# The spatial unit's input projection by seven products per two-by-two block of quarters, with sums of weight quarters made during the attention

## The chip, the cores and the metric

The kernel runs on one core of one Trainium2 chip. The metric is the device time of one execution in microseconds; the kernel before takes 3173.32 us, the median of three runs (3173.29 to 3175.74). TensorE multiplies matrices (PE in the profile, its weight loads PEld), VectorE is DVE, ScalarE is ACT, GpSimd is POOL, and SyncE (SP) issues most DMAs.

## The reference, cut to what matters

A two-layer decoder trunk on 2048 rows of 1024 numbers. The first layer is attention, the second a gated unit:

```python
def sgu_layer(x, norm_g, w_in, ln_g, ln_b, w_s, b_s, w_out):
    h = rms_norm(x, norm_g)
    proj = jnp.einsum('bsd,de->bse', h, w_in)          # 1024 -> 3 x 2048
    u, v, g = jnp.split(proj, [SGU_WIDTH, 2 * SGU_WIDTH], axis=-1)
    u = jax.nn.gelu(u, approximate=False)
    v = layer_norm(jax.nn.gelu(v, approximate=False), ln_g, ln_b)
    ...
    sp = jnp.einsum('gts,bnsgc->bntgc', ws, vg) + b_s.T[None, None, :, :, None]
    y = u * sp * jax.nn.silu(g)
    return x + jnp.einsum('bse,ed->bsd', y, w_out)
```

All numbers are 32-bit. A product of two matrices is made of three: each operand is split into a high half (a cast, on ScalarE) and a low half (the rest, a subtraction on VectorE; `split`, lines 92 and 93), and high x high, high x low and low x high are added up in PSUM.

## The kernel before, in words

**First layer.** `project` (L291) makes the projection of the attention in eight units of columns, 16 row blocks of 128 rows each; its 24 matmuls per block (L310 to L312) are mixed by hand with those of the attention of the unit before. From the second unit on the split rows `hT` come back from DRAM by two DMAs per block (L206) into four half buffers, so loads are issued more than a block ahead. GpSimd normalizes and rotates queries and keys of every second block (`norm_rope`) and stores them (L281). Then come two passes of output projection. In the second (`out_second`, L730 on), per row block: the residual sum `x1` (L713), its squares (ScalarE, L761), the factor of the norm from them by some ten tiny ops on VectorE (`factor`, L106), and one block later four transposes per half (`turn`, L738) and a store to `h2_s`.

**Second layer**, from L815 on: four groups of four row blocks. A group loads its turned rows (`load_h`) and splits them; then comes v: four chunks of 512 columns, each with eight [128x512] weight pieces in four slots of 512 KB (`load_w`: one of three raw buffers `wr`, cast, subtraction; two sets of four split slots `wh0`, `wl0` and `wh1`, `wl1`), used by all four blocks, 24 matmuls each (`proj`, L112). The norm factor of the row is applied by the activation that reads PSUM (`scale=r2`). `bn_stats` and, per block, `bn_aggr` and a chain of tiny ops give `rstd` and `nmu`. Then, per chunk: u with the mixing (L920 to L940: two VectorE ops make `vn`, a split makes `vs`, six matmuls `pp` mix rows), the gate (L952 to L958), and the output projection from four slots of the output weights (L970 to L973), with four transposes per block ahead of it.

**Order.** TensorE executes in the order in which the program is written. The other engines' orders, SP's and GpSimd's DMA queues among them, are set by a scheduler at build time, by its own durations and the written order as priority; on the chip every engine and queue then executes in that fixed order and waits at semaphores. Where all buffers of a tag are in use, the instruction that writes next waits for the release, and what stands behind it on its engine waits too.

## Time and profile before

| | |
|---|---|
| Median of three runs | 3173.32 us |
| The profiled execution's own time | 3177.81 us |
| Its span, first to last instruction | 3176.0 us |
[...]
| Busy: TensorE, VectorE, ScalarE, GpSimd | 97%, 58%, 45%, 21% of the span |
| HBM read and written | 391.79 MB, 100.93 MB |

The first layer lasts to about 1695 us, the second from there to the end. A busy TensorE is one with a matmul in flight; neighbouring matmuls overlap, so what one costs is the distance of two starts, not its duration. Idle time of an engine is printed with what ended it ("<-DVE wl L93" is the instruction of L93 on VectorE that wrote `wl`).

### The profile page before, as it was taken

How to read it: one execution, taken by the hardware profiler on the slowest of the kernel's cores; microseconds unless marked ns; L12 is line 12 of the kernel's file. 1: busy time of each engine (PE TensorE's matmuls, PEld its weight loads, DVE VectorE, ACT ScalarE, POOL GpSimd, SP SyncE). 2: the span in 40 equal slices, each digit the busy share in tenths (PEclk: the TensorE clock that was granted, in tenths of full speed). 3: DMA queues.
4: the chain of work that ended last, by engine and by line, in shares of the span. 5: the costliest groups of instructions: out<-in, count | busy, mean ns of one | idle time of the engine just before them, and what ended most of it. 6: DMA issues, size and time to landing. Idle time of an engine off the chain costs nothing.

```text
span 3176.0 us, 45128 instructions
## 1 busy us (share of the span) xinstructions
PE 3070.1 (97%) x15816; PEld 2594.8 (82%) x15816; DVE 1839.8 (58%) x4414; ACT 1425.6 (45%) x2676; POOL 660.3 (21%) x1771
## 2 busy tenths in 40 slices
PE   8889999999999999989999999999999999999999
PEld 6679787988879787977887888888888888888887
DVE  5435785467655785457876655436555555446553
ACT  5535565465555565544534333333333343334332
POOL 6434433454244533431121000000000000000000
PEclk9899999999999999999999999999999999999999
DMA  9976848585576848476356423343224423243321
GB/s 377 323 200 184 243 148 229 154 229 184 174 211 189 238 149 234 148 200 204 127 192 234 160 80 106 123 156 93 94 92 143 143 94 99 93 151 115 106 80 60
DMA packets 302660, 520.87 MB, mean 164 GB/s; under 512 B 57056, under 2 KB 147296, under 8 KB 302432
## 3 DMA queue, kind: packets, MB, share of 16 engines
q1 hardware_dynamic: 285280, 463.17, 47.4%
q0 software_dynamic: 17152, 54.80, 4.6%
q8 instruction: 125, 2.05, 0.3%
q14 instruction: 103, 0.84, 0.1%
HBM read 391.79 MB, written 100.93 MB: 155 GB/s over the span
## 4 chain that ended last, share of the span: by engine, by line
PE 86%; DMA 6%; DVE 4%; ACT 2%; issue 2%; POOL 1%; SPq 0%; DVEq 0%; ACTq 0%; POOLq 0%
PE pm L115 11%; PE pm L114 11%; PE pm L116 11%; PE pm L310 6%; PE pm L312 5%; PE pm L311 5%; PE po L972 4%; PE po L970 4%; PE po L971 4%; PE po L627 4%; PE pu L531 4%; PE s_ps L488 3%; PE sd_ps L590 2%; PE sd_ps L591 2%; DMA hT<-hts 2%; PE pT L507 2%
## 5 line engine op out<-in xcount | busy, mean ns | idle before, releaser
L114 PE MATMUL pm<-wh,hT 128*128 128x512 f32 x1536 | 600.5, 391 | 1.7 <-ACT wh L92 1.7
L115 PE MATMUL pm<-wl,hT 128*128 128x512 f32 x1536 | 599.5, 390 | 2.2 <-DVE wl L93 2.2
L116 PE MATMUL pm<-wh,hT 128*128 128x512 f32 x1536 | 598.4, 390 | 0.0
L310 PE MATMUL pm<-wh,hT 128*128 128x512 f32 x1024 | 448.7, 438 | 47.5 <-DMA hT<-hts 31.2
L311 PE MATMUL pm<-wl,hT 128*128 128x512 f32 x1024 | 406.5, 397 | 3.2 <-POOL wl L93 3.2
L312 PE MATMUL pm<-wh,hT 128*128 128x512 f32 x1024 | 407.9, 398 | 0.5 <-DVE hT L221 0.5
L92 ACT CAST wh<-wr 128x1024 fp32r<-128x1024 f32 (+1 forms) x276 | 277.6, 1020 | 277.3 <-PE po L972 124.3
L93 DVE TENSOR_TENSOR wl<-wr,wh 128x1024 fp32r<-128x1024 f32 (+1 forms) x272 | 321.0, 1193 | 113.9 <-ACT wh L92 105.8
L114 PEld LDWEIGHTS pm<-wh,hT 128*128 128x128 f32 x1536 | 289.0, 188 | 60.3 <-ACT wh L92 2.4
L116 PEld LDWEIGHTS pm<-wh,hT 128*128 128x128 f32 x1536 | 288.8, 188 | 60.6
L115 PEld LDWEIGHTS pm<-wl,hT 128*128 128x128 f32 x1536 | 289.1, 188 | 59.7 <-DVE wl L93 2.9
L310 PEld LDWEIGHTS pm<-wh,hT 128*128 128x128 f32 x1024 | 197.8, 193 | 69.9 <-issue 24.4
L312 PEld LDWEIGHTS pm<-wh,hT 128*128 128x128 f32 x1024 | 194.7, 190 | 47.0 <-DVE hT L221 3.0
L311 PEld LDWEIGHTS pm<-wl,hT 128*128 128x128 f32 x1024 | 197.6, 193 | 21.5 <-POOL wl L93 5.3
L597 ACT ACTIVATE sd<-sd,nmd 128x128 f32<-128x128 f32 (+15 forms) x128 | 154.0, 1203 | 132.3 <-DVE nmd L593 127.4
L970 PE MATMUL po<-wh,yT 128*128 128x512 f32 x512 | 203.6, 398 | 0.0
L972 PE MATMUL po<-wh,yT 128*128 128x512 f32 x512 | 199.8, 390 | 0.0
L971 PE MATMUL po<-wl,yT 128*128 128x512 f32 x512 | 199.6, 390 | 0.0
L973 DVE TENSOR_TENSOR acc<-po,acc 128x512 f32<-128x512 f32 x128 | 88.1, 689 | 159.9 <-PE po L972 159.9
L499 ACT ACTIVATE sm<-sm,um 128x256 f32<-128x256 f32 (+1 forms) x256 | 116.1, 486 | 143.3 <-DVE um L497 143.0
L531 PEld LDWEIGHTS pu<-vt,pTs 128*128 128x128 f32 x1200 | 160.0, 191 | 16.2 <-ACT u L534 2.6
L497 DVE CUSTOM_DVE_ANT_0 sm<-s_ps,masks 128x256 f32<-128x256 f32 (+1 forms) x224 | 84.9, 416 | 151.7 <-PE s_ps L488 151.6
(180 smaller groups left out, 5726.7 us busy)
## 6 DMA issues: line engine op xcount, KB each, us to landing
hT<-hts SPq DMA_DIRECT2D x224, 512.0 KB, 4.2
wr<-in_sgu_w_in SPq DMA_DIRECT2D x192, 512.0 KB, 4.6
wr<-in_sgu_w_out SPq DMA_DIRECT2D x64, 512.0 KB, 4.4
hts<-hT SPq DMA_DIRECT2D x32, 512.0 KB, 7.4
vg<-vg SPq DMA_DIRECT2D x64, 256.0 KB, 2.7
qk<-raw POOLq DMA_DIRECT2D x64, 256.0 KB, 4.7
rows<-qk SPq DMA_DIRECT2D x64, 256.0 KB, 4.6
kk<-kk SPq DMA_DIRECT2D x64, 256.0 KB, 5.5
```

The lines of the kernel that those rows point to most:

```text
L92: A.copy(hi, src)
L93: return E.tensor_sub(lo, src, hi.bitcast(F32))
L114: T.matmul(pm, hT[:, 0, dc], w[dc][0], start=dc == 0, stop=False)
L115: T.matmul(pm, hT[:, 0, dc], w[dc][1], start=False, stop=False)
L116: T.matmul(pm, hT[:, 1, dc], w[dc][0], start=False, stop=dc == DC - 1)
L310: T.matmul(pm, z[:, 0, k], w[dc][0], start=dc == 0, stop=False)
L311: T.matmul(pm, z[:, 0, k], w[dc][1], start=False, stop=False)
L312: T.matmul(pm, z[:, 1, k], w[dc][0], start=False, stop=dc == DC - 1)
L531: T.matmul(pu[:, g0 % 4 + t], pTs[:, t, P * q:P * q + P], vt[pat][:, vb, 65 * i:65 * i + 65], start=q == 0, stop=q == nk - 1)
L970: T.matmul(po, yT[:, 0, i], wo2[i][0][:, es], start=i == 0, stop=False)
L971: T.matmul(po, yT[:, 0, i], wo2[i][1][:, es], start=False, stop=False)
L972: T.matmul(po, yT[:, 1, i], wo2[i][0][:, es], start=False, stop=i == 3)
```

## The change

**Products.** A group's projection of v, u or gate is seen as a product of two-by-two quarters: rows are a pair of blocks (j is 0 or 1: blocks j and j+2), the depth has two halves of 512, and columns are 512 from either half of the 2048. Seven products of quarters with sums and differences of quarters (Strassen's, in a form with few sums) take the place of eight. `strassen` is called for v, u and gate and for two column quarters `cc`; per product it runs twelve matmuls for each j. Partial results are added up in PSUM (`x`, `y`) where a product is part of two results; a copy (ScalarE) and a sum (VectorE) per result finish them (L923, L927, L944).

**Sums of weights.** Four of the seven weight operands are sums of quarters. `quarter_sums` makes them on GpSimd in the first layer, 48 pieces, one behind every second row block of `project` from the second unit on: two loads (SP), four subtractions, one store to DRAM (`t_s`). It has one buffer, `tq`; for it raw weight buffers of the first layer go from five to three. A load is placed behind the last issued `hT` load in priority.

**Sums of rows.** `rows_sums` makes seven split operands per pair of blocks; four sums on GpSimd. `hr` has one buffer for a pair of blocks. Rows of the next group are made during the output projection. Rows are scaled by their norm factor before they are turned, so the activations lose their scale.

**Others.** Split slots are one ring of five (`WS`) for all weights. The subtraction of `vs` goes to GpSimd. One chain gives `rstd` for four blocks. The output projection takes two times four blocks after each `cc`. The turning of the last two row blocks moves into the first group's output projection, and that of the others one block later.

```diff
@@ -32,8 +32,8 @@
-HT_BUFS, W_BUFS, WR_BUFS, SM, PTS, UM = 4, 9, 5, 5, 4, 4
-DWR, VS_BUFS = 3, 2
+HT_BUFS, W_BUFS, WR_BUFS, SM, PTS, UM = 4, 9, 3, 5, 4, 4
+DWR, WS, VS_BUFS = 3, 5, 2
...
-LATE = 1
+LATE = 2
@@ -280,6 +275,25 @@
+            def quarter_sums():
+                for m in (1, 0, 2):
+                    for kc in range(4):
+                        for e in range(0, 1024, 256):
+                            t = w1.tile([P, 2, 2, 256], F32, name="tq", tag="tq", bufs=1)
+                            for h in range(2):
+                                src = a["sgu_w_in"][512 * h + P * kc:512 * h + P * kc + P, SW * m:SW * m + SW]
+                                with tc.issue_after(loaded[-1].ins):
+                                    nc.sync.dma_start(t[:, h], src.rearrange("p (h e) -> p h e", h=2)[:, :, e:e + 256])
+                            G.tensor_sub(t[:, 0, 0], t[:, 0, 1], t[:, 0, 0])
+                            G.tensor_sub(t[:, 0, 1], t[:, 1, 1], t[:, 0, 1])
+                            G.tensor_sub(t[:, 1, 1], t[:, 1, 1], t[:, 0, 0])
+                            G.tensor_sub(t[:, 1, 0], t[:, 1, 0], t[:, 1, 1])
+                            G.dma_start(t_s[m][kc][:, :, e:e + 256], t.rearrange("p a b e -> p (a b) e"))
+                            yield
@@ -313,6 +327,8 @@
+                    if not first and b % 2:
+                        next(sums, None)
@@ -753,16 +769,17 @@
                     if b < NB - LATE:
                         factor(w1, b)
+                        for n in range(2):
+                            A.activation(x1[n], x1[n], AF.Copy, scale=r2[b][:, 0:1])
@@ -821,37 +838,35 @@
+            def slot(src, n):
+                nonlocal last_load
+                shape = [P, n, 1024 // n]
+                raw = tile_(shape, F32, "wr", DWR)
+                last_load = nc.sync.dma_start(raw, src)
+                hi = tile_(shape, F32R, "wh", WS)
+                lo = tile_(shape, F32R, "wl", WS)
+                split(hi, lo, raw)
+                return [(hi[:, k], lo[:, k]) for k in range(n)]
@@ -868,111 +883,272 @@
+            A11, A12, S2, S1, S3, S4, A22 = range(7)
+            PRODUCTS = ((A11, "B", 0, 0), (A12, "B", 4, 0), (S2, "T", 3, 0), (S1, "T", 0, 0),
+                        (S3, "T", 1, 0), (S4, "B", 4, 1024), (A22, "T", 2, 0))
...
+            def strassen(ht, m, cc, sum_to, done):
+                x, y, u2, o = {}, {}, {}, {}
+                def product(j, acc, i, w, start):
+                    z = ht[j][i]
+                    for kc in range(4):
+                        for k, (p, q) in enumerate(((0, 0), (0, 1), (1, 0))):
+                            T.matmul(acc, z[:, p, kc], w[kc][q], start=start and kc == k == 0, stop=kc == 3 and k == 2,
+                                     skip_group_check=True)
+                def taken(j, r, c, p):
+                    o[j] = sum_to(j, r, c)
+                    A.copy(o[j], p)
+                def summed(j, r, c, p, q=None):
+                    z = sum_to(j, r, c) if q is not None else o[j]
+                    V.tensor_add(z, p, z if q is None else q)
+                    done(j, r, c, z)
+                for n, (i, *which) in enumerate(PRODUCTS):
+                    w = quarter(m, cc, *which)
+                    for j in range(2):
...
+                        product(j, x[j] if n in (0, 2, 4, 6) else y[j], i, w, n in (0, 1, 3))
+                        if n == 0:
+                            taken(j, 0, 0, x[j])
+                        elif n == 1:
+                            summed(j, 0, 0, y[j])
+                        elif n == 2:
+                            u2[j] = tile_([P, 512], F32, "u2", 2)
+                            A.copy(u2[j], x[j])
+                        elif n == 3:
+                            taken(j, 1, 1, y[j])
+                        elif n == 4:
+                            summed(j, 1, 1, x[j])
+                        elif n == 5:
+                            summed(j, 0, 1, y[j], u2[j])
+                        elif n == 6:
+                            done(j, 1, 0, x[j])
+                        yield
+            def rows_sums(gi, j):
...
+                hr = tile_([P, 4, 4, P], F32, "hr", 1)
...
+                parts(A11, a11)
+                parts(A12, a12)
...
+                G.tensor_add(s1, a21, a22)
...
+                G.tensor_sub(s2, s1, a11)
...
+                mv = w1.tile([P, GB, 2], F32, name="mv", tag="mv", bufs=2)
                 for b in blocks:
...
+                    V.bn_aggr(mv[:, b % GB], st6[b])
+                rstd = w1.tile([P, GB], F32, name="rstd", tag="rstd", bufs=2)
+                rsqrt(w1, rstd, mv[:, :, 1], 1.0, LN_EPS, GB)
...
-                        split(vs[:, 0], vs[:, 1], vn)
...
+                        split(vs[:, 0], vs[:, 1], vn, G)
+                        yield
...
+                    for n, _ in enumerate(strassen(ht, 0, cc, new_sum, u_done)):
+                        if 3 <= n < 11:
+                            next(mixes[n - 3], None)
+                        if 1 <= n < 9:
+                            next(mixes[n - 1])
```

Three places show how the order moves. The first is VectorE where the second layer starts: `r_14_81`, `r_15_82` are the factors of the last row blocks, `hT` and `h` split rows, `wl` low halves of weights. Before:

```order
L110 TENSOR_SCALAR r_14_81<-r_14_81 128x1
L713 TENSOR_TENSOR x_19297<-pmo,x_19297 128x512
L740 TENSOR_TENSOR h2T<-pth,gn 128x512 x4
L93 TENSOR_TENSOR hT_19392<-hr,hT_19392 128x1024
L93 TENSOR_TENSOR wl_19391<-wr,wh_19377 128x1024
```

After:

```order
L729 TENSOR_TENSOR x_19666<-pmo,x_19666 128x512
L756 TENSOR_TENSOR h2T<-pth,gn 128x512 x2
L110 TENSOR_TENSOR r_15_82<-r_15_82 128x1
...
L86 SCALAR_TENSOR_TENSOR r_15_82<-rs_t,r_15_82 128x1
L93 TENSOR_TENSOR h_19729<-hr,h_19729 128x512
L93 TENSOR_TENSOR h_19730<-hr,h_19730 128x512
L93 TENSOR_TENSOR h_19735<-hr,h_19735 128x512
L93 TENSOR_TENSOR h_19732<-ct,h_19732 128x512
L93 TENSOR_TENSOR wl<-wr,wh 128x1024
L93 TENSOR_TENSOR h_19731<-ct,h_19731 128x512
```

The factors of the last two blocks and four splits of rows now stand between the last output sum and the first low half of weights.

The second is VectorE where the second group goes from v to u; `mv`, `rs_v`, `rs_t` and `rstd` are the chain of the layer norm, `vn` the normalized v, `ct` a sum of products. Before:

```order
L893 BN_STATS st_22080<-vv_22079 128x6
L904 BN_AGGR mv<-st_22080 128x2
...
L80 TENSOR_SCALAR rstd<-rs_v 128x1
L920 SCALAR_TENSOR_TENSOR vn<-vv_22079,nmu,ln 128x512
...
L86 SCALAR_TENSOR_TENSOR rstd<-rs_t,rstd 128x1
L921 SCALAR_TENSOR_TENSOR vn<-vn,rstd,ln 128x512
L893 BN_STATS st_22138<-vv_22137 128x6
L93 TENSOR_TENSOR vs<-vn,vs 128x512
```

After:

```order
L1032 BN_STATS st_22696<-vv_22695 128x6
L93 TENSOR_TENSOR wl<-wr,wh 128x1024
L1042 BN_AGGR mv<-st_22696 128x2
...
L86 SCALAR_TENSOR_TENSOR rstd<-rs_t,rstd 128x4
L927 TENSOR_TENSOR ct<-y,ct 128x512
...
L93 TENSOR_TENSOR wl<-wr,wh 128x1024
L86 SCALAR_TENSOR_TENSOR rstd<-rs_t,rstd 128x4
L927 TENSOR_TENSOR ct<-y,ct 128x512
L1065 SCALAR_TENSOR_TENSOR vn<-vn,rstd,ln 128x512 x2
```

The end of the chain, and with it `vn`, moved behind two sums that wait for TensorE's second product. On TensorE the mixing of this group (`pp`) follows that product's second half (`h_22495`):

```order
L918 MATMUL y<-wl,h_22495 128x512
L918 MATMUL y<-wh,h_22495 128x512
L1073 MATMUL pp<-vs,wsp 128x256
L1074 MATMUL pp<-vs,wsp 128x256
L1075 MATMUL pp<-vs,wsp 128x256
...
L918 MATMUL x<-wh,h_22358 128x512
```

Before, 24 matmuls of u for the first row block stand ahead of the first mixing, and those of the first block need only that block's chain.

The third is SP's queue at the end of the second unit of the first layer; `hT` are the split rows of blocks 14, 15 and then 0. Before:

```order
L206 DMA hT<-hts_14_111 128x1024
L206 DMA hT<-hts_14_112 128x1024
L206 DMA hT<-hts_15_113 128x1024
L206 DMA hT<-hts_15_114 128x1024
L437 DMA y_0_147<-gt 32x8x64
L327 DMA vg_127<-vg 128x2x256
...
L206 DMA hT<-hts_0_83 128x1024
```

After:

```order
L201 DMA hT<-hts_14_111 128x1024
L201 DMA hT<-hts_14_112 128x1024
L288 DMA tq<-in_sgu_w_in 128x2x256 x2
L201 DMA hT<-hts_15_113 128x1024
L201 DMA hT<-hts_15_114 128x1024
L343 DMA vg_127<-vg 128x2x256
L288 DMA tq<-in_sgu_w_in 128x2x256
L453 DMA y_0_147<-gt 32x8x64
...
L288 DMA tq<-in_sgu_w_in 128x2x256
L201 DMA hT<-hts_0_83 128x1024
```

Loads of `tq` now stand between loads of `hT`; the first of each pair waits for the store of the piece before.

## Rows read from the trace of the kernel before

**Rows 1.** The page's head and its part 1: busy us, share, instructions.

```profile
span 3176.0 us, 45128 instructions
...
PE 3070.1 (97%) x15816; PEld 2594.8 (82%) x15816; DVE 1839.8 (58%) x4414; ACT 1425.6 (45%) x2676; POOL 660.3 (21%) x1771
```

**Rows 2.** Stretches: stretch, us, busy of each engine (instructions), granted clock, DMA share, GB/s.

```profile
100.00:1150.00 1050.00, 987.65 (x5656) 852.40 (x5656) 632.39 (x1946) 575.63 (x1280) 440.55 (x1238) 0.98 0.68 202
...
1800.00:2000.00 200.00, 200.00 (x937) 166.85 (x936) 109.36 (x137) 73.02 (x103) 0.00 (x0) 1.00 0.29 90
```

**Rows 3.** Timeline of TensorE, second layer: start, duration, instruction; idle before it.

```profile
1999.84 0.39 PE L114 MATMUL pm<-wh,hT 128*128 128x512 f32 x1
...
2004.60 0.28 PE L932 MATMUL pp<-vs,wsp 128*128 128x256 f32 x1
...
2005.31 0.40 PE L114 MATMUL pm<-wh,hT 128*128 128x512 f32 x1
```

**Rows 4.** The page's part 5, the projection's first matmul: busy, mean ns, idle before.

```profile
L114 PE MATMUL pm<-wh,hT 128*128 128x512 f32 x1536 | 600.5, 391 | 1.7 <-ACT wh L92 1.7
```

**Rows 5.** Groups by form on VectorE, 1800 to 3150 us.

```profile
L93 DVE TENSOR_TENSOR wl<-wr,wh 128x1024 fp32r<-128x1024 f32 x232 | 280.8, 1222 | 102.9 <-ACT wh L92 95.9
L973 DVE TENSOR_TENSOR acc<-po,acc 128x512 f32<-128x512 f32 x120 | 82.6, 689 | 146.3 <-PE po L972 146.3
...
L920 DVE SCALAR_TENSOR_TENSOR vn<-vv,nmu,ln 128x512 f32<-128x512 f32 x59 | 44.2, 749 | 1.1
...
L86 DVE SCALAR_TENSOR_TENSOR rstd<-rs_t,rstd 128x1 f32<-128x1 f32 x36 | 5.5, 157 | 0.7
```

**Rows 6.** The same on ScalarE.

```profile
L92 ACT CAST wh<-wr 128x1024 fp32r<-128x1024 f32 x232 | 240.5, 1052 | 254.6 <-PE po L972 124.3 <-DMA wr<-in_sgu_w_in 83.8 <-PE pm L116 40.7
...
L92 ACT CAST vs<-vn 128x512 fp32r<-128x512 f32 x61 | 37.9, 621 | 0.0
```

**Rows 7.** Timeline of all engines where the second layer starts.

```profile
1692.82 0.40 PE L710 MATMUL pmo<-wh,yT 128*128 128x512 f32 x1
...
1694.57 0.19 ACT L761 ACTIVATION_READ_ACCUMULATOR sqx<-x 128x1 f32 x1
...
1696.69 0.50 PE L114 MATMUL pm<-wh,hT 128*128 128x512 f32 x1 [1.44 <-ACT wh L92]
...
1699.68 0.63 PE L114 MATMUL pm<-wh,hT 128*128 128x512 f32 x1
...
1700.11 0.63 PE L115 MATMUL pm<-wl,hT 128*128 128x512 f32 x1
```

**Rows 8.** The page's part 6, DMA issues: KB each, us to landing.

```profile
wr<-in_sgu_w_in SPq DMA_DIRECT2D x192, 512.0 KB, 4.6
...
qk<-raw POOLq DMA_DIRECT2D x64, 256.0 KB, 4.7
```

**Rows 9.** Groups by form on GpSimd, whole span.

```profile
L267 POOL TENSOR_TENSOR raw<-raw,rs 128x512 f32<-128x512 f32 x64 | 67.1, 1049 | 5.0
...
L434 POOL TENSOR_TENSOR gt<-gt,u 128x512 f32<-128x512 f32 x16 | 18.9, 1201 | 5.8 <-DVE u L430 5.8
```

**Rows 10.** Timeline of VectorE and GpSimd in the first layer.

```profile
265.19 4.71 POOL L427 TENSOR_TENSOR u<-u,dm 128x1024 f32<-128x1024 f32 x2 [4.20 <-DVE dm L425]
...
268.07 2.92 DVE L430 TENSOR_TENSOR u<-u 128x1024 f32<-128x1024 f32 x1 [1.03 <-POOL u L427]
```

**Rows 11.** TensorE's waits from 100 to 1400 us: total, times, longest.

```profile
PE pm L310 <- DMA hT<-hts: 31.2, 10, 14.7
```

**Rows 12.** Timeline of a weight slot's load, cast and subtraction.

```profile
2089.51 3.09 SPq L849 DMA_DIRECT2D wr<-in_sgu_w_in  x3
...
2093.22 1.05 ACT L92 CAST wh<-wr 128x1024 fp32r<-128x1024 f32 x1 [1.28 <-DMA wr<-in_sgu_w_in]
...
2094.30 1.23 DVE L93 TENSOR_TENSOR wl<-wr,wh 128x1024 fp32r<-128x1024 f32 x1 [1.50 <-ACT wh L92]
```

**Rows 13.** The stretch 400 to 800 us, line 310 alone.

```profile
400.00:800.00 400.00, 125.57 (x285) 54.63 (x285) 1.00 0.63 187
```

## The prediction

> **What bounds the kernel now.** I read the page's first lines, then the table of stretches, then the timeline of TensorE in the last stage, the groups by form there, and last the waits. The span is 3176.0 us and TensorE is busy for nearly all of it [rows 1]. The table splits this: from 100 to 1150 us, the first layer, TensorE is busy 987.65 of 1050 us, GpSimd 441, and DMA engines have a share of 0.68; from 1800 us on, in the second layer, TensorE is busy 200.00 of 200 us, VectorE about half, GpSimd not at all [rows 2]. So the second layer has one bound, the number of TensorE instructions. "Mean 391 ns" of the group at L114 is not their price, since matmuls overlap: 21 of them lie between the first and second row of [rows 3], 4.76 us, so one costs 0.2267 us. The six of the spatial mixing after them cost 0.71 us.

> **What is removed.** The input projection at L114 to L116 has 3 x 1536 = 4608 matmuls [rows 4]. Per group of four row blocks and half of the columns of one of v, u, gate there will be seven products x two pairs of row blocks x 12 matmuls = 168, where there were 192; x 24 that is 4032. 576 x 0.2267 = **130.6 us** less. The output projection (1536), the mixing and the transposes stay.

> **What is added on TensorE's neighbours.** Now four slots of input weights (512 KB each) serve 96 matmuls; after, two serve the 24 of a product. So 24 x 14 = 336 slots are split in place of 192; the 64 of the output weights stay. Per slot ScalarE needs 1.05 us, VectorE 1.22 [rows 5, 6]. New too are 144 copies and 144 sums of [128x512]. VectorE in the stage after: 400 x 1.222 + about 584 ops x 0.689 (sums, output sums, bn_stats, gate, splits) + 192 x 0.749 = 1035 us [rows 5] of about 1341: 77%. ScalarE has less. On average all of it is hidden by TensorE. What it costs is at the places where VectorE's order puts something late.

> 1. Start of the stage, **+10**. [...] After: VectorE first does the factors of two row blocks, 25 tiny ops in two interleaved chains (13 to 25 x 0.157 [rows 5], I take 3 us), then four splits of [128x512] (2.8), then the first low half of weights (1.2): second matmul at about 1701.8, 3 us later than at present. The second row pair needs the one buffer of `hr`, free after three more splits and two slots (4.5), then a load of about 4.6 [rows 8] and a cast: 1711.5, while the first pair's 12 matmuls end at 1705. That is 6.5 us idle and 1.6 more at half clock; 1 us of such waits goes. Bounds 0 to 16.

> 2. From v to u, **+23**. At present each row block has its own chain to `rstd`. After, one chain serves four, and VectorE's order puts its end, and `vn`, behind the sum (L927) of the second product's second row pair; TensorE's order puts the first mixing matmuls right behind that product. So TensorE waits: 0.2 to the sum, 0.6 sum, 0.75 vn, 0.62 high half on ScalarE [rows 5, 6], 1.2 low half on GpSimd, where the nearest rows for [128x512] have 1.20 and 1.05 us [rows 9]: 3.4 us, and 1.6 at half clock. In the first group two slots lie between as well (2.8). 3 x 5.0 + 7.8 = 22.8. Nothing else can fill it, as TensorE runs in order. Bounds 8 to 36.

> 3. First half of u, **+12**. VectorE has 12 of the group's 16 mixes here: after the sum, 20 ops of 0.75, seven slots, two sums: 24.9 us, and with eight low halves on GpSimd at 1.2 that stop it, 34.5. TensorE wants the last slot 8.5 half products of 2.72, eight mixings of 0.71 and the wait of term 2 later, 33 us in all; as `vn` also waits for its two buffers I take 3 us late, x 4. Whether GpSimd stops it: in [rows 10] a VectorE op with two SBUF operands began at 268.07 under a GpSimd op that ended at 269.90, and took 2.92 us where one of its shape takes 1.22 [rows 5]; 269.90 + 1.1 is its end. [...] Bounds 0 to 30.

> 4. From gate to output, second half, three groups, **+7**. The splits of the next group's rows stand between the last weight slots; adding 0.65 per op from the sum of the sixth product, the fourth slot comes about 1 us late and the third block's transposes 1.5. Bounds 0 to 18.

> 5. Between the two column quarters of the output, **+6**. Five buffers hold four slots and one more, where there were two sets of four; the last slot is cast and subtracted after its buffer is free, about 0.7 us late, eight times. Bounds 0 to 12.

> 6. First layer, **+7**. 48 loads and 48 stores of 512 KB are 50 MB over some 1085 us, 46 GB/s on 202 [rows 2]: 23% more. TensorE waits 31.2 us for `hT` now [rows 11]; 23% of it is 7. GpSimd gets 192 subtractions of about 0.6 (half of [rows 9]) and 48 stores of about 0.8: 150 us, from 42% to 56% busy. A load of `tq` waits on SP's queue for the store before it; behind it stand `hT` loads, issued more than one row block ahead; a block takes 11.2 us (285 matmuls of L310, eight to a block, in 400 us [rows 13]), which hides about 10 us. If that cover were gone, a store's 4.7 us [rows 8] would show 47 times, 221 us. Raw weight buffers fall from five to three; three are loaded and split well within a row block, so 0. Bounds -5 to 40.

> Weight slots: three raw buffers. At present one goes from issue at 2089.51 over cast at 2093.22 to the end of the subtraction at 2095.53, 6.0 us [rows 12], so a slot every 2.0 us against 2.72 needed (12 x 0.2267). I put it at 0; the queues on ScalarE and VectorE may add 2.2 us before it counts.

> **Sum.** 10 + 23 + 12 + 7 + 6 + 7 = 65. The profiled execution's own time is 3177.8: 3177.8 - 130.6 + 65 = 3112.2. That execution lies 4.5 above the median of 3173.3, so **3108 us**.

> **Rivals.**
> - TensorE stays packed: only the start costs, 3173.3 - 130.6 + 10 = 3053. For it: every stretch of the stage is now 200.00 of 200. Against: the waits of term 2 stand in the order.
> - VectorE becomes the bound in u and elsewhere, each GpSimd op of the stage stopping it: in u of a group VectorE has 28 slots, 12 sums and 48 ops of the mixes, 78.4 us, and 16 x 1.2 against TensorE's 336 matmuls and 16 mixings, 87.5; 10 late, four times 40 in place of term 3: 3136.
> - Slower: the ring of three raw slots decides. Load, cast and subtraction queue behind in-order waits; each us of its cycle above 8.2 costs 336/3 = 112 us. From 8.8 us on the gain is gone; at 9.5 the time is 3108 + 146 = 3254. For it: VectorE at 77%, in u near 90%. Against: 6.0 now, and three slots of lead in the split buffers.

> **How the numbers follow.** Forecast 0.60, packed 0.15, VectorE 0.17, ring 0.08. The range goes from 3060 (near the packed case) to 3155 (past the VectorE case, with term 6 at its bound); the ring lies outside. A change below 0.2%, 6 us, can't be told from none. Faster 0.92, same 0.01, slower 0.07.

> **What would show it.** 4032 matmuls in the projection; at the first mixing of each group TensorE idle 3 to 6 us behind GpSimd's `vs`; one wait of some 6 us for the second pair at the start; few waits inside v and gate. [...]

## The result: 0.8% slower, and the profile after

The kernel after takes 3201.39 us (median of four runs, 3196.29 to 3203.04), the kernel before 3174.53 in the same comparison. The ratio is 1.0081, 95% interval 1.0063 to 1.0098. The forecast was 3108, range 3060 to 3155: sign and size are both wrong.

The execution profiled after took 3202.59 us. First the page's head, two of its groups of the projection, and two DMA rows. They answer to [rows 1, 4, 8].

```profile
span 3200.8 us, 45580 instructions
...
PE 3004.0 (94%) x15240; PEld 2509.5 (78%) x15240; DVE 2124.1 (66%) x4506; ACT 1657.8 (52%) x3036; POOL 1001.9 (31%) x2103
...
L918 PE MATMUL x<-wh,h 128*128 128x512 f32 x1536 | 506.8, 400 | 11.2 <-ACT h L92 6.1
...
L918 PE MATMUL y<-wh,h 128*128 128x512 f32 x1152 | 374.8, 394 | 0.0
...
tq<-in_sgu_w_in SPq DMA_DIRECT2D x96, 256.0 KB, 5.0
t<-tq POOLq DMA_DIRECT2D x48, 512.0 KB, 4.7
```

The two groups with `wh` make 2688 matmuls, those with `wl` half as many: 4032, as planned. 576 fewer instructions run on TensorE (15816 to 15240), and the span is still 24.8 us longer. So the first question is where in the program. The stretches of the kernel after (columns as in [rows 2]); the first line is the whole first layer:

```profile
0.00:1738.00 1738.00, 1610.40 (x9014) 1379.70 (x9015) 1064.68 (x3229) 907.81 (x1980) 841.12 (x2004) 0.97 0.75 231
...
545.41:587.58 42.17, 31.74 (x148) 26.83 (x148) 18.35 (x50) 19.60 (x40) 20.96 (x54) 0.88 0.88 262
587.58:638.75 51.17, 51.17 (x330) 46.42 (x329) 20.98 (x89) 25.82 (x68) 28.57 (x74) 1.00 0.68 211
```

The same of the kernel before:

```profile
0.00:1695.00 1695.00, 1596.80 (x9032) 1369.17 (x9032) 1052.92 (x3260) 890.47 (x1955) 658.34 (x1768) 0.98 0.67 208
...
525.12:560.63 35.51, 29.07 (x147) 24.39 (x147) 18.69 (x50) 19.43 (x40) 14.45 (x48) 1.00 0.91 252
560.63:611.80 51.17, 51.17 (x329) 46.16 (x327) 20.89 (x89) 24.61 (x65) 20.41 (x60) 1.00 0.57 170
```

The last transposition of the first layer starts at 1694.98 before and 1738.18 after: **the first layer lost 43.2 us.** In it TensorE is idle 98.2 us before (1695 - 1596.80) and 127.6 after; the other 13.8 us are busy time, at a mean clock of 0.97 instead of 0.98. The lines after the first are row blocks 4 to 7 and 8 to 11 of the fourth unit. Blocks 8 to 11 last 51.17 us in both kernels, with GpSimd at 28.57 us instead of 20.41. Blocks 4 to 7 last 6.7 us longer. In them DMA engines had a share of 0.91 already before.

From there to the last matmul the program became only 18.5 us shorter (1476.9 to 1458.4). I split that by the distances of matmul starts; a gap here is what a distance has over the matmul's own 0.2267 us, or over that of a shorter one, where it is more than 0.3:

| Second layer, us | before | after | difference |
|---|---|---|---|
| 576 matmuls removed at 0.2267 each, 16 transpositions added | | | -128.8 |
| gaps over 0.3 us between matmuls | 5.2 | 73.8 | +68.6 |
| excess of matmuls at half clock (granted 0.50) | 1.3 | 15.2 | +13.9 |
| excess of matmuls at full clock (granted 1.00) over 0.2267 | 9.4 | 36.9 | +27.5 |

The gaps, as the waits of TensorE from 1720 us on list them (total, times, longest):

```profile
PE pp L1073 <- ACT vs L92: 24.5, 4, 7.0
PE y L1145 <- DVE yT L93: 10.1, 3, 3.4
PE x L918 <- DVE wl L93: 8.5, 5, 5.9
PE pp L1074 <- POOL vs L93: 6.4, 6, 1.7
PE x L918 <- ACT h L92: 6.1, 1, 6.1
```

Four waits per program for `vs`, one for each group, are the step from v to u. At the second group TensorE's timeline shows one:

```profile
2214.55 0.39 PE L918 MATMUL y<-wh,h 128*128 128x512 f32 x1
2221.25 0.58 PE L1073 MATMUL pp<-vs,wsp 128*128 128x256 f32 x1 [6.32 <-ACT vs L92]
2223.52 0.58 PE L1074 MATMUL pp<-vs,wsp 128*128 128x256 f32 x1 [1.69 <-POOL vs L93]
...
2224.76 0.63 PE L918 MATMUL x<-wh,h 128*128 128x512 f32 x1
2225.18 0.63 PE L918 MATMUL x<-wl,h 128*128 128x512 f32 x1
```

The last two rows start 0.42 us apart, at a granted clock of 0.50; this lasts to 2229. VectorE and GpSimd in the same stretch:

```profile
2217.99 1.23 DVE L93 TENSOR_TENSOR wl<-wr,wh 128x1024 fp32r<-128x1024 f32 x1
2219.20 0.68 DVE L927 TENSOR_TENSOR ct<-y,ct 128x512 f32<-128x512 f32 x1
2219.80 1.41 DVE L1065 SCALAR_TENSOR_TENSOR vn<-vn,rstd,ln 128x512 f32<-128x512 f32 x2
...
2221.28 3.42 POOL L93 TENSOR_TENSOR vs<-vn,vs 128x512 fp32r<-128x512 f32 x2 [128.92 <-ACT vs L92]
...
2223.50 1.75 DVE L1064 SCALAR_TENSOR_TENSOR vn<-vv,nmu,ln 128x512 f32<-128x512 f32 x1 [1.15 <-POOL vs L93]
...
2226.82 1.61 POOL L93 TENSOR_TENSOR vs<-vn,vs 128x512 fp32r<-128x512 f32 x1 [2.12 <-ACT vs L92]
2227.21 1.77 DVE L1065 SCALAR_TENSOR_TENSOR vn<-vn,rstd,ln 128x512 f32<-128x512 f32 x1
```

Between TensorE's last matmul of the product and `vn` stand low halves of weights and two sums. `vn` takes 0.75 us where GpSimd is quiet and 1.75 to 1.77 under or against a `vs`. At the start TensorE's timeline is:

```profile
1743.28 0.80 PE L918 MATMUL x<-wh,h 128*128 128x512 f32 x1 [4.83 <-ACT wh L92]
1749.95 0.79 PE L918 MATMUL x<-wl,h 128*128 128x512 f32 x1 [5.87 <-DVE wl L93]
...
1761.00 0.80 PE L918 MATMUL x<-wh,h 128*128 128x512 f32 x1 [6.14 <-ACT h L92]
```

That is three waits, where [rows 7] has one of 1.44.

### The profile page after: what moved, and what is told of

Same layout as the page of the kernel before. It is cut to its first block, busy times and chain, and to the rows that moved or that the text cites. A ratio compares the mean times of both kernels' runs of the same rounds, so it can differ in the third digit from the quotient of the medians.

```text
span 3200.8 us, 45580 instructions
## 1 busy us (share of the span) xinstructions
PE 3004.0 (94%) x15240; PEld 2509.5 (78%) x15240; DVE 2124.1 (66%) x4506; ACT 1657.8 (52%) x3036; POOL 1001.9 (31%) x2103
## 4 chain that ended last, share of the span: by engine, by line
PE 64%; issue 15%; DMA 8%; DVE 8%; ACT 3%; POOL 1%; SPq 1%; DVEq 0%; ACTq 0%; POOLq 0%
PE x L918 10%; PE y L918 7%; PE pm L324 5%; PE pm L326 5%; PE pm L325 5%; PE pu L547 4%; PE po L643 3%; PE s_ps L504 3%; PE y L1144 2%; PE y L1145 2%; PE y L1143 2%; PE pT L523 2%; PE pmo L724 2%; PE pmo L726 2%; PE pmo L725 2%
## 5 line engine op out<-in xcount | busy, mean ns | idle before, releaser
L918 PE MATMUL x<-wh,h 128*128 128x512 f32 x1536 | 506.8, 400 | 11.2 <-ACT h L92 6.1
L324 PE MATMUL pm<-wh,hT 128*128 128x512 f32 x1024 | 453.8, 443 | 50.7 <-DMA hT<-hts 31.8
L325 PE MATMUL pm<-wl,hT 128*128 128x512 f32 x1024 | 411.1, 401 | 2.8 <-POOL wl L93 2.7
L326 PE MATMUL pm<-wh,hT 128*128 128x512 f32 x1024 | 411.9, 402 | 0.2
L918 PE MATMUL y<-wh,h 128*128 128x512 f32 x1152 | 374.8, 394 | 0.0
L918 PEld LDWEIGHTS x<-wh,h 128*128 128x128 f32 x1536 | 294.3, 192 | 79.2 <-ACT h L92 6.7
L918 PE MATMUL x<-wl,h 128*128 128x512 f32 x768 | 306.2, 399 | 8.6 <-DVE wl L93 8.5
L324 PEld LDWEIGHTS pm<-wh,hT 128*128 128x128 f32 x1024 | 200.8, 196 | 73.9 <-issue 22.6
L326 PEld LDWEIGHTS pm<-wh,hT 128*128 128x128 f32 x1024 | 197.5, 193 | 46.6 <-DVE hT L216 1.2
L918 PE MATMUL y<-wl,h 128*128 128x512 f32 x576 | 225.9, 392 | 0.0
L325 PEld LDWEIGHTS pm<-wl,hT 128*128 128x128 f32 x1024 | 200.3, 196 | 21.6 <-POOL wl L93 4.8
L1145 PE MATMUL y<-wh,yT 128*128 128x512 f32 x512 | 203.9, 398 | 10.1 <-DVE yT L93 10.1
L1143 PE MATMUL y<-wh,yT 128*128 128x512 f32 x512 | 207.8, 406 | 0.0
```

Of the source, the lines that this page charges most:

```text
L324: T.matmul(pm, z[:, 0, k], w[dc][0], start=dc == 0, stop=False)
L325: T.matmul(pm, z[:, 0, k], w[dc][1], start=False, stop=False)
L326: T.matmul(pm, z[:, 1, k], w[dc][0], start=False, stop=dc == DC - 1)
L918: T.matmul(acc, z[:, p, kc], w[kc][q], start=start and kc == k == 0, stop=kc == 3 and k == 2, skip_group_check=True)
L1143: T.matmul(po, yT[:, 0, i], wo2[i][0][:, es], start=i == 0, stop=False)
L1145: T.matmul(po, yT[:, 1, i], wo2[i][0][:, es], start=False, stop=i == 3)
```

## The experiments

Each ratio is to the kernel before, run on the same chip in the same comparison; all edits are to the kernel after unless said otherwise.

### Where the first layer loses

**The sums left out.** Removed: the call of `quarter_sums`; sum operands read plain quarters instead.

```diff
-                    if not first and b % 2:
-                        next(sums, None)
...
-                        src = t_s[m][2 * q:2 * q + 2, :, k, 512 * cc:512 * cc + 512].rearrange("k p e -> p k e")
+                        src = win[:, 2 * q:2 * q + 2, SW * m + 512 * cc:SW * m + 512 * cc + 512]
```

> Leaves out the sums of weight quarters: nothing of them is loaded, subtracted or stored during the attention, and the products that used a sum multiply by a plain quarter of the same size, loaded from the input. The numbers of matmuls, loads and splits in the second layer stay. Theory (the first layer's 43 us, 1695.0 to 1738.2 us at its last transposition, are the price of GpSimd's quarter sums): the last transposition is back at 1693 to 1700 us, the second layer stays at some 1462 us, the time is 3155 to 3165 us. Rival (the loss comes from the slower start, 343 against 377 GB/s in the first slice, or from the schedule of the rest): the first layer still ends after 1725 us and the time stays over 3185 us.

Measured: 3161.93 us, ratio 0.9954 (0.9936 to 0.9972). The first layer ends at 1697.45, within 2.5 us of before. The second takes 1458.6, as in the kernel after. So some 41 us belong to the sums, and nothing of the second layer's loss does. What in them costs this is seen next.

**Loads one step ahead of the subtractions.** GpSimd waits for the loads of `tq`; perhaps TensorE's waits follow from that.

```diff
+                            yield
                             G.tensor_sub(t[:, 0, 0], t[:, 0, 1], t[:, 0, 0])
...
-                    if not first and b % 2:
+                    if not first:
```

> The two loads of a piece of quarters are issued one row block before GpSimd subtracts them, instead of directly ahead of it; the amount of work is the same. Theory (what costs in the first layer is GpSimd standing still behind the loads, 131 + 20 us in 48 pieces, with the norms and stores of the rows queued behind, which the transpositions of the rows then wait for): GpSimd's wait for these loads falls below 40 us, TensorE's wait for the stored rows from 26.6 to about 10 us, the first layer ends 20 to 35 us earlier, the time is 3165 to 3182 us. [...]

Measured: 3193.88, ratio 1.0058 (1.0039 to 1.0076); the first layer ends at 1724.67, 13.5 earlier. GpSimd's first subtraction in the kernel after, and in this one, over the first layer:

```profile
L289 POOL TENSOR_TENSOR tq<-tq 128x256 f32<-128x256 f32 x48 | 35.3, 736 | 131.0 <-DMA tq<-in_sgu_w_in 130.9
```

```profile
L290 POOL TENSOR_TENSOR tq<-tq 128x256 f32<-128x256 f32 x48 | 39.2, 817 | 94.6 <-DMA tq<-in_sgu_w_in 94.2
```

The wait fell by only 37 us and the gain is a third of the 41, so the theory holds in part at most. TensorE's waits from 117 to 1406 us in the kernel after show what else there is:

```profile
PE pm L324 <- DMA hT<-hts: 31.8, 7, 12.3
PE ptq L368 <- DMA rows<-qk: 26.6, 6, 8.0
```

`hT`, on which my term 6 rested, is at 31.8 (31.2 in [rows 11]). `rows`, the normalized queries and keys read back, are at 26.6; without the sums they are at 9.3. Their transfer, issue to landing, in the DMA issues of the kernel before and of the kernel after:

```profile
rows<-qk SPq DMA_DIRECT2D x64, 256.0 KB, 4.6
```

```profile
rows<-qk SPq DMA_DIRECT2D x64, 256.0 KB, 5.9
```

**Sums at every second block from 0 on**, so that the end of a unit is free:

```diff
-                    if not first and b % 2:
+                    if not first and b in (0, 2, 4, 6, 8, 10, 12):
```

> The changed kernel with the pieces of quarter sums placed at row blocks 0, 2, 4, ..., 12 of a unit's projection (7 a unit) instead of at 1, 3, ..., 15 (8 a unit), so that none stands in GpSimd's queue just ahead of the norms and the store of the unit's last rows, which the next attention unit's first transpositions wait for. Theory (TensorE's 48.8 us of idle time ahead of the transpositions of the rows, 24.3 before the change, come from those last pieces): it falls below 30 us and the first layer ends 15 to 28 us earlier than 1738 us. Rival (the amount of work and of traffic counts, not its place): the idle time stays over 42 us and the first layer ends after 1730 us.

Measured: 3194.39, ratio 1.0052 (1.0036 to 1.0068); the first layer ends at 1731.5. Blocks 4 to 7 kept their loss (0.6, 0.7, 2.4 and 0.6 us a unit; in the kernel after 0.5, 1.1, 2.7 and 0.6), so the place at the end of a unit isn't the cause. The chain of waits of this kernel shows in one row what TensorE waits for there:

```profile
543.64 10.99 DMA rows<-qk
```

GpSimd's timeline just before it:

```profile
543.50 0.77 POOL L293 DMA_DIRECT2D t<-tq  x1 [0.31 <-POOL rs_t L84]
```

The 256 KB of `rows` took 10.99 us behind a store of 512 KB issued 0.14 us earlier. The same load took 7.3 us in the kernel before, more than the median of 4.6 over all of them. In the kernel after, SyncE's queue adds to it. The next load of `rows` in these blocks, in the chain of waits of before and of after:

```profile
526.15 7.82 DMA rows<-qk
```

```profile
544.48 7.81 DMA tq<-in_sgu_w_in
...
552.30 9.76 DMA rows<-qk
```

It is issued only when a load of `tq` has landed (SyncE's waits have 1.3 us for that one), and it then takes 2 us longer. TensorE waits 8.9 us for `rows` between 540 and 566 us, where it waited 2.5 in the same blocks before: nearly all of the 6.7 that these blocks lost.

**Sums away from blocks 1 to 6**: if the full DMA stretch is the cause, its loss goes with the sums.

```diff
-                    if not first and b % 2:
+                    if not first and b in (0, 7, 9, 10, 12, 13, 15):
```

> The changed kernel with the pieces of quarter sums placed behind row blocks 7, 9, 10, 12, 13, 15 and 0 of a unit's projection, so that none is loaded or stored during blocks 3 to 7, in which the next unit's rows, keys and queries are brought in. Theory (the first layer's loss is contention for the DMA engines in these blocks: their mean busy share is 0.75 to 1.05 there before the change, and blocks 4 to 7 together take 4.9 us longer a unit with the sums, all others together 1.1 us): these blocks lose under 1 us a unit, the first layer ends near 1700 us instead of 1738, the time is 3163 to 3172 us. Rival (GpSimd's own work delays the rows wherever it stands): the blocks 4 to 7 keep 3 to 5 us of loss a unit and the time stays over 3190 us.

Measured: 3180.85 (ten runs), ratio 1.0017 (1.0007 to 1.0028). The first layer ends at 1715.3, 22.9 earlier, and blocks 4 to 7 lose 0.0. In the fourth unit these blocks last, in this kernel:

```profile
540.53:574.80 34.27, 29.35 (x150) 24.75 (x150) 18.26 (x49) 19.28 (x39) 15.89 (x46) 1.00 0.96 287
```

34.27 us, where the kernel after has 42.17. So more than half of the loss depends on where the pieces fall. GpSimd's subtractions moved along with the transfers, and no run moves one alone; that it is the transfers rests on the two loads of `rows` above, which take 6.2 and 7.4 us here. The end near 1700 that was expected is missed by 15 us. What remains, 3.4 us a unit, stands at blocks 0 (1.4), 12 (0.6) and 15 (0.8).

**Sums away from the end of the unit too**, on top of the best version below:

```diff
-                    if not first and b in (0, 7, 9, 10, 12, 13, 15):
+                    if not first and b in (1, 7, 8, 9, 10, 11, 12):
```

> The kernel 'best' with the sums' pieces behind row blocks 1 and 7 to 12 instead of 0, 7, 9, 10, 12, 13 and 15. Theory (what is left of the loss in the first layer, 3.2 us a unit, stands in blocks 15 and 0, 1.0 and 1.7 us, where a piece meets the loads of the next unit): these two fall to 0.5 and 0.8 us as without sums, and the first layer ends 8 to 14 us earlier than 1714 us. Rival (pieces in successive blocks wait for the one buffer, and SyncE's queue with them): the loss moves to blocks 8 to 13 and the first layer ends within 4 us of 1714 us or later.

Measured: 3146.74 (3144.97 to 3151.97), ratio 0.9912 (0.9897 to 0.9926); the first layer ends at 1710.2. Block 15 loses nothing, block 0 went from 1.7 to 1.1, but blocks 9, 12 and 13 lose 0.6, 0.7 and 0.5: 2.9 us a unit instead of 3.2. This lies between the theories; the rest of some 12 us stays open.

### From v to u

**The mixing two half products later**, so that other matmuls lie between the layer norm and `pp`:

```diff
-                        if 3 <= n < 11:
-                            next(mixes[n - 3], None)
-                        if 1 <= n < 9:
-                            next(mixes[n - 1])
-                        while pend and pend[0][0] <= n - 3:
+                        if 5 <= n < 13:
+                            next(mixes[n - 5], None)
+                        if 3 <= n < 11:
+                            next(mixes[n - 3])
+                        while pend and pend[0][0] <= n - 5:
                             pend.pop(0)[1]()
+                    while pend:
+                        pend.pop(0)[1]()
```

> The normalisation and the mixing of a pair of column quarters are each placed two products' passes later among the seven products of u. Theory (TensorE waits at the first mixing of each group because the variance chain, two normalising operations and GpSimd's low half follow the last product of v directly: 8.4, 8.6, 7.8 and 8.0 us, with 7 to 10 us at half clock behind each): these four waits vanish, the second layer is 35 to 42 us shorter, the time 3158 to 3167 us. Rival (VectorE is the bound there, so the wait moves to a weight half or to the end of u's products): as much idle time turns up at the products' lines or at the gate and the time stays over 3190 us.

Measured: 3184.94, ratio 1.0035 (1.0019 to 1.005). The second layer takes 1442.0 us, 16 less than in the kernel after and not 35 to 42. The waits of this kernel from 1720 us on:

```profile
PE y L1147 <- DVE yT L93: 13.7, 6, 3.4
PE pp L1074 <- POOL vs L93: 8.2, 5, 1.9
...
PE pp L1073 <- ACT vs L92: 2.5, 2, 1.6
```

Of the waits for `vs` 10.7 us of 30.9 remain. TensorE now waits for GpSimd's `vs`, and its gaps at the output grew by some 6 us. The mechanism is confirmed; its worth was under half of what I expected.

### The matmul that became longer

In the products a matmul of 512 columns starts 231.3 ns after the one before, in the output 232.8; before it was 227.2 and 227.5. In the products of the kernel after, the mean distance with an engine idle (under 5% of the distance) and with it busy (over half of it) is 231.4 and 230.8 ns for ScalarE, 230.2 and 231.5 for VectorE, 231.4 and 230.9 for GpSimd; below and above the same DMA shares it is 232.1 and 231.2.

**Fewer waits at semaphores.** Theory: a matmul that has to look at a semaphore costs more.

```diff
-                    for kc in range(4):
-                        for k, (p, q) in enumerate(((0, 0), (0, 1), (1, 0))):
+                    for kc in (2, 3, 0, 1):
+                        for k, (p, q) in enumerate(((0, 1), (0, 0), (1, 0))):
```

> Within a pass the four 128-row pieces of a weight quarter are taken in the order 2, 3, 0, 1 and the low half first, so that TensorE waits for the second slot at once and not again in the middle: 395 waits at the product line instead of 646. Theory (each semaphore wait costs TensorE its lead, and the next 6 to 7 matmuls start 231 to 233 ns apart instead of 227): the mean distance in the products falls from 231.3 to about 229.5 ns, 7 us of the time, while waits for weights may grow by 0 to 5 us. Rival (memory traffic or another engine's use of the memory slows the matmuls): the mean distance stays at 231 ns or above.

Measured: 3202.41, ratio 1.009 (1.0072 to 1.0107). The product line has 395 waits in place of 646, and the distance is still 231.3 ns. The theory fell.

**A different place in SBUF.** In the kernel after, four tiles `st6` of 96 bytes each (384 in a partition) lie between the rows of a group's first row pair (stationary) and the weights (moving), and between the output's `yT` and the weights; the rows of the second pair (`h1` in the kernel) lie behind `st6`, with the weights. Before, the `st6` tiles lay ahead of all rows and weights. Theory: the place of one operand against the other sets the distance. First, `st6` padded to 128 bytes, 512 in all:

```diff
-                     ("th", 2, [P, 512], F32), ("st6", GB, [P, 4, 6], F32)] +
+                     ("th", 2, [P, 512], F32), ("st6", GB, [P, 4, 8], F32)] +
...
-                    st6[b] = tile_([P, 4, 6], F32, "st6", GB)
+                    st6[b] = tile_([P, 4, 8], F32, "st6", GB)[:, :, 0:6]
```

> The only edit: a small tile of statistics is padded from 96 to 128 bytes a partition (four of them, 512 instead of 384), so that the tiles that lie behind it in SBUF, the weight halves among them, have the same address modulo 512 bytes as the stationary rows that lie before it (192 and 192, where the changed kernel has 192 and 64). No instruction is added, removed or moved. Theory (the distance between matmuls of 512 columns, 231.3 ns in the products and 232.8 in the output projection against 227.2 and 227.5 before the change, comes from that relative address): it falls to 226.7 to 228 ns in both, the second layer is 20 to 27 us shorter, the time 3173 to 3182 us. Rival (the distance comes from the shape of the products, passes of 12 matmuls, or from the busier memory): it stays above 230.5 ns and the time within 5 us of 3201.

Measured: 3184.73 (seven runs), ratio 1.0027 (1.0016 to 1.0039). TensorE's timeline holds 192 matmuls from the first of these rows to the second, 191 distances, in the kernel after:

```profile
2251.07 0.39 PE L918 MATMUL y<-wh,h 128*128 128x512 f32 x1
...
2295.26 0.39 PE L918 MATMUL x<-wh,h 128*128 128x512 f32 x1
```

and padded:

```profile
2251.90 0.40 PE L918 MATMUL y<-wh,h 128*128 128x512 f32 x1
...
2295.22 0.39 PE L918 MATMUL x<-wh,h 128*128 128x512 f32 x1
```

44.19 / 191 = 0.2314 us, and 43.32 / 191 = 0.2268. The excess of the second layer fell from 36.9 to 15.7 us (9.4 before), and the layer takes 1442.4 us. That is 16 us less where 20 to 27 were expected, since gaps and half clock grew by some 5.

**The same fault put into the kernel before:** an unused tile of 384 bytes ahead of the weights' second set.

```diff
-                    ("wh1", 4, [P, 2, 512], F32R), ("wl1", 4, [P, 2, 512], F32R)):
+                    ("pad", 1, [P, 96], F32), ("wh1", 4, [P, 2, 512], F32R), ("wl1", 4, [P, 2, 512], F32R)):
```

> The kernel before the change with one unused tile of 384 bytes a partition laid ahead of one of its two sets of weight buffers; that set, which every second group of weight columns uses, then lies at 32 modulo 512 bytes against the rows' 160, the other set at 160. Nothing else is changed. Theory (relative address): the matmuls on the shifted set go to 231 to 234 ns apart, those on the other stay at 227; the time rises by 10 to 18 us to 3184 to 3192. Rival (the address plays no part): both sets stay at 227 ns and the time at 3172 to 3178 us.

Measured: 3197.59 (two runs), ratio 1.0068 (1.0048 to 1.0088), and the second layer takes 1493.9, 17 us more. From column to column the distance alternates; each pair of rows below has 96 matmuls between:

```profile
1724.50 0.40 PE L114 MATMUL pm<-wh,hT 128*128 128x512 f32 x1
...
1746.89 0.39 PE L114 MATMUL pm<-wh,hT 128*128 128x512 f32 x1
...
1768.66 0.40 PE L114 MATMUL pm<-wh,hT 128*128 128x512 f32 x1
```

22.39 / 96 = 0.2332 us with one set of weights, 21.77 / 96 = 0.2268 with the other. The median is nearly 6 us above the range expected. So in this kernel the place of the weights sets the distance: only the shifted set has the longer one, and nothing else of the change is in it.

**How far apart counts.** Two further places (one run each): `st6` of 192 bytes, 768 in all, and the padded version with 32 bytes more.

```diff
-                     ("th", 2, [P, 512], F32), ("st6", GB, [P, 4, 6], F32)] +
+                     ("th", 2, [P, 512], F32), ("st6", GB, [P, 4, 12], F32)] +
```

```diff
-                     ("th", 2, [P, 512], F32), ("st6", GB, [P, 4, 8], F32)] +
+                     ("th", 2, [P, 512], F32), ("st6", GB, [P, 4, 8], F32), ("pad", 1, [P, 8], F32)] +
```

> The changed kernel with the tile of statistics padded to 192 bytes, so that the weight halves lie at 448 modulo 512 bytes against the stationary rows' 192: 256 apart. If only an equal address modulo 512 lets the matmuls run 227 ns apart, they are 230 to 234 ns apart here; if 256 is enough, 227 ns as with equal addresses.

> The changed kernel with the padded tile and 32 bytes more behind it: the weight halves lie at 224 modulo 512 bytes against the stationary rows' 192. If the distance of the matmuls depends on equal addresses modulo 64 or more, they are 230 to 234 ns apart; if 32 bytes make no difference, 227 ns.

Measured: 256 bytes further the distances are 227.2 and 228.1 ns (3188.73 us), as padded to 512. 32 bytes further they are 230.2 and 233.2 (3200.37 us). So in the products the distance is 227.2 ns with 512 or 768 bytes put in, 230.2 with 32 more than 512, and 231.3 with 384. Other steps weren't tried.

These are means over both row pairs, and the pairs differ. The first two rows below are of a pass of the first pair, nine matmuls apart, the other two of the pass of the second pair on the same weights, in the kernel with 32 bytes more:

```profile
2143.64 0.40 PE L918 MATMUL y<-wl,h 128*128 128x512 f32 x1
...
2145.74 0.39 PE L918 MATMUL y<-wl,h 128*128 128x512 f32 x1
...
2146.42 0.39 PE L918 MATMUL y<-wl,h 128*128 128x512 f32 x1
...
2148.46 0.39 PE L918 MATMUL y<-wl,h 128*128 128x512 f32 x1
```

2.10 / 9 = 0.2333 us, and 2.04 / 9 = 0.2267. The weights are the same ones at the same place, so it isn't the place of the weights by itself: only the first pair's rows lie 32 bytes off against them. One thing doesn't fit. In the kernel after the first pair's mean distance is 233.0 ns, but the second pair's is 229.5 and not 227, although its rows lie with the weights. Why stays open.

### The start of the second layer

**A second buffer for the rows of the first group**, on top of the best version below: `hr` of the second row pair gets the space of `vv`.

```diff
-                hr = tile_([P, 4, 4, P], F32, "hr", 1)
+                hr = (tile_([P, SW], F32, "vv3", 1).rearrange("p (q c t) -> p q c t", q=4, c=4) if b == 1 else
+                      tile_([P, 4, 4, P], F32, "hr", 1))
```

> The kernel 'best' with the second row pair's raw tile of the very first group taken from a buffer that is not yet in use, so that its two loads need not wait for the first pair to be split and are issued ahead of the weight loads. Theory (the third wait at the start of the second layer, 7.4 us in 'best' and 6.4 in the changed kernel, is that load standing in SyncE's queue behind four weight loads, the last of which waits for a free raw slot): the third wait falls below 2 us and the time by 5 to 9 us. Rival (VectorE, which has 14 splits of rows before it, is what ends the start): the wait moves to a weight half, the sum of the three waits stays at 17 to 20 us and the time within 3 us of 'best'.

Measured: 3153.57, ratio 0.9927 (0.9911 to 0.9944), no gain; the waits at the start are 18.0 us with and without the edit, two of them (11.1 and 6.9) in place of three. SyncE's timeline shows that the edit didn't do its work:

```profile
1728.46 0.80 SPq L961 DMA_DIRECT2D vv<-h  x2
1729.30 14.86 SPq L865 DMA_DIRECT2D wr<-in_sgu_w_in  x4
```

The load, now early in SyncE's order, was issued only at 1728.46, and the weight loads stood behind it; without the edit they start at 1703.01. That it waited for the first layer to release that part of SBUF is an inference. Whether the one buffer of `hr` causes the third wait stays open.

### Edits together

**Three edits**: padded, mixing later, sums at every second block from 0.

> The changed kernel with three of these edits at once: the padded tile, the mixing two passes later, the quarter sums away from the end of a unit. If each gives what it is thought to give alone (24, 18 and 20 us), and they do not overlap, the time is 3135 to 3145 us, below the kernel before. If the second layer is bound by VectorE, the first two overlap and it stays over 3150 us.

Measured: 3162.59, ratio 0.9955 (0.994 to 0.997). The first layer ended at 1726.7: spacing the sums had been expected to give more.

**Padded, mixing later, sums away from blocks 1 to 6:**

> The changed kernel with the padded tile, the mixing two passes later, and the sums' pieces outside blocks 3 to 7. If the three causes are separate, the first layer ends near 1700 us, the second takes 1431 us, and the time is 3132 to 3142 us. If what the sums cost only moves to other blocks, it stays over 3155 us.

Measured: 3151.83, ratio 0.9929 (0.9913 to 0.9946), layers of 1714.5 and 1427.1. Ten us above the upper end expected; the first layer still ends 17 us later than without the sums.

**The two edits on top of it together** (sums at blocks 1 and 7 to 12, rows first):

> Both of these edits in 'best': if they are separate, the time is the sum of their two differences to 'best', 3130 to 3142 us.

Measured: 3146.86, ratio 0.9911 (0.9895 to 0.9928). Nothing beyond the sums' new place. The version with that alone is as fast and simpler: 3146.74, some 0.9% better than the kernel before and 1.7% better than the kernel after.

## Why the prediction was wrong, step by step

The forecast's sum was -130.6 + 65; the two profiled executions differ by +24.8. So 90 us are to be found. All six terms at their upper bounds would have given 3195, still below the result: a size that was off does not explain it alone.

- **What is removed: the count held, the price of what stays did not.** 576 matmuls less were forecast at -130.6; by the counted matmuls it is -128.8. But the step took 0.2267 us as a property of the matmul. The 5567 matmuls of 512 columns left in the stage each got some 5 ns longer, **+27.5 us**. No term had it. Some 21 us of it are the tiles' changed places, shown by the padded `st6` (-21) and by the shifted weights in the kernel before (+17); the other 6 stay open.
- **Term 6, the first layer: +7 forecast, +43.2 measured**, over its upper bound of 40. This is the largest miss, and the step that failed is the cover. The forecast raised the waits for `hT` by 23%, from 46 GB/s on a mean of 202 over 1050 us [rows 2]. `hT` is issued more than a block ahead, and that cover held (31.8 us of waits for 31.2). The transfer without cover was `rows`, in blocks where the share was near 0.9 already, with loads of `tq` ahead of it on SyncE: 26.6 us of waits, 9.3 without the sums. Shown by leaving the sums out (41 us are theirs) and by moving the pieces away from those blocks (22.9 us come back). Of the 29.4 us more that TensorE is idle, these waits are some 17; the rest was not traced.
- **Term 2, v to u: +23 forecast; gaps of 32.8 us**, and 2.4 at half clock behind each (nine matmuls 0.2 late, six of the mixing 0.1): some 42, over the bound of 36. The mechanism was the forecast's, the list of what stands before `vn` was not: two sums and low halves of 1.23 where it priced one sum. 3.4 us were forecast per wait (6.2 in the first group), 8.2 were measured on average. Later mixing confirms the place.
- **Term 1, the start: +10 forecast**, gaps of 18.6 against 5.2, so +13.4, and half clock behind two of them to 1754 and 1765. It is at the upper bound of 16. The second and third wait were named; the first (4.83, ScalarE's casts of rows ahead of `wh`, one of them 0.99 late behind a sum on GpSimd) was not.
- **Term 3, u against GpSimd: +12 forecast, at most 1 us of TensorE's waits measured.** VectorE is slowed in the trace: at the second group `vn` takes 0.75 us alone and 1.75 to 1.77 against a `vs`; a `vs` itself takes 1.64 on average (1.2 was taken). That each of these subtractions costs VectorE its full length was my estimate, and no run shows it. The step that failed is the next one: the queue worked out had VectorE 3 us late in each group, but its delay reached almost no matmul, so it had more slack in u than that.
- **Terms 4 and 5, the output: 13 forecast, some 18 measured.** 73.8 - 18.6 - 32.8 leaves 22.4, of which nearly 5 are short waits in v and u. Three waits for `yT` of 3.4 us, where the next group's rows are split, are term 4; term 5's short waits for `wl` are nine of at most 0.2; the rest stands at the transpositions.
- **Half clock: +13.9** in the second layer. The forecast had 1.6 us per wait at the start and in term 2: in the kernel before the granted clock is 0.50 from 1699.20 to 1701.90 us, where eight matmuls run, 0.43 us apart instead of 0.23. About 2.4 us came behind each long wait.
- **The rivals.** The ring of three raw slots, the only one on the slower side, did not occur: in the projection TensorE waits for `wl` five times in the whole stage, 8.5 us, and 5.9 of them at the start. VectorE was no bound either, with 73% busy from 1760 to 3150 us. The slow outcome had a chance of 0.07 for the wrong reason.

So the parts of the miss are: first layer 36, distance 27.5, terms 1 and 2 with their half clock about 25, output and the short waits in v and u with their own about 11, less 12 for term 3, and 2 in the count. The waits that were forecast happened, but for term 3, at 1.3 to 1.8 times their price. What decided the sign were the first layer, which the forecast called covered, and the distance, which it took as fixed.

## What to carry to other kernels

A DMA share averaged over a stage did not say here where new transfers fit: it was 0.67 over the first layer before, and 0.91 in blocks 4 to 7 of its fourth unit, where the time was lost. So look at it block by block, and put transfers where the short-lead loads are not. When tiles are added, removed or resized, compare the distance of matmul starts before and after. In the products here it went from 227.2 to 231.3 ns, and 512 or 768 bytes in place of 384 between two operands brought it back to 227.2; that other layouts behave so was not shown, so measure. Some 5 ns on 5567 matmuls are as much as a fifth of the work saved here. And where one chain comes to serve four blocks, list every instruction between its last input and its first use in the engine's order before pricing the wait.

## What the runs showed of the hardware that I had not expected

A transfer of 256 KB took 10.99 us when a 512 KB store had been issued 0.14 us before it, in row blocks where the kernel after has a DMA share of 0.88. The same load of the kernel before took 7.3 us at a share of 0.91 over these blocks; the medians of all loads of `rows` are 4.6 before and 5.9 after.
